# Interleaved B projections, reordered vector work, one gate-weight ring, later transposes and paced FFN loads in an encoder block

One Trainium2 chip, all 8 cores, every core on its own slice of the tokens with the same program. The metric is the device time in microseconds of the slowest core. Every kernel and experiment below gave correct results against the reference.

This program has two states. In the slow one the cores of one die, sometimes of both, run at a visibly lower granted TensorE clock and the time is up to 17% longer.

## The reference

A post-norm encoder block on x of 4 x 4096 x 2048, cut to what matters:

```python
qa, ka, va, qb, kb, vb, ga, gb = jnp.split(x @ w_in, split_pts, axis=-1)
# A: 8 query heads, 2 key/value heads, RMS-normed and rotated, full bidirectional softmax
out_a = _gqa_blocks(qa * scale, ka, va)                       # (B, S, 1024)
# B: 12 heads in 3 groups of dilation 1, 4, 16; 129 keys per query, ALiBi bias;
#    the 3 groups' heads are combined by their softmax denominators
out_b = _dilated_window_attention(qb * scale, kb, vb)         # (B, S, 512)
gate_a = jax.nn.sigmoid(ga + b_gate[0])
gate_b = jax.nn.sigmoid(gb + b_gate[1])
mixed = (gate_a * (out_a @ w_proj_a) + gate_b * (out_b @ w_proj_b)) @ w_out
x = _layer_norm(ALPHA * x + mixed, ln1_g, ln1_b)
h = jax.nn.silu(x @ w_ffn_gate) * (x @ w_ffn_up)              # hidden width 5632
x = _layer_norm(ALPHA * x + h @ w_ffn_down, ln2_g, ln2_b)
```

## The kernel before

The program is written as one list of operations; a helper gives each its waits, and each engine runs its part in list order. So "where a line stands in the list" is the whole schedule. `fil` is a queue of filler matmuls that TensorE takes between the steps of an attention. A matmul writes into one of the program's PSUM banks, and the bank is free again when VectorE or ScalarE has copied its result out ("evacuated" it). A "ring" is a set of buffers taken in turn. A "cold" or half-speed matmul is one that the trace shows at about twice its usual pitch after a gap. The parts, with cuts marked:

```python
# ---- stage 2: attention A (512 steps); filler: B's key, value and query projections
SG = [...4 x [128, 512]...];  KS = at("KS", 184, [128, 3072], BF16)      # staging of values / of keys and queries
def fbank():                       # the filler's two PSUM banks, taken in turn
    b = bank[6 + fb_n[0] % 2]
    fb_n[0] += 1
    return b
def qk_head(wsrc, nt_list, dst, key, dil):         # one key or query head, tiles of 512 tokens
    ...
    s.mm(bk[:, 0:n], w[:, ...], XB_[tb][:, kc, 0:n], kc == 0, kc == 15)
    if kc == 15:
        s.copy("dve", KS[:, tb * 512:tb * 512 + n], bk[:, 0:n])          # cut: the dilated form
        if tb == nt_list[-1][0]:
            s.dma("sp", dst[:, 0:tot], KS[:, 0:tot], wk=[key])           # the store must leave KS before the next head
for g in (2, 1, 0):                                 # four key heads, then all value tiles of the group
    for hh in range(4):
        qk_head(...)
    v_group(g)
...                                                 # then twelve query heads
# at the end of each of the 32 blocks of 16 steps, between filler tiles:
pd = fbank()
s.mm(pd, ones[:, :], AC[blk3 % 2][:, 0:512])        # softmax denominator
s.actf(RD[:, :], pd, AF.Ln)
s.actf(RD[:, :], RD[:, :], AF.Exp, scale=-1.0)
s.tt("dve", QA[h3][:, ...], bank[4 + blk3 % 2], RD[:, :], ALU.mult)

# ---- stage 3: attention B, 48 "quads" (4 per head of dilation 16, then dilation 4 and 1 in turn)
for t in range(NQ + LAGB):
    if t < NQ:
        ... 8 score matmuls into st; bias by VectorE (one or two stt) ...
        ex = s.actf(pb[:, :], st[:, :], AF.Exp)
        pb4 = pb[:, :].rearrange("p (a e c) -> p a e c", a=4, e=2)
        s.tt("dve", DS[t % 3]..., pb4[:, :, 0, :], pb4[:, :, 1, :], ALU.add)      # follows its exp at once
    fil.run_to(min(1.0, (t + 0.5) / NQ))                                          # gate tiles as filler
    if t >= LAGB:
        ... value matmuls of quad t-2 into num, denominators into den ...
        else:                                                                     # dilation 1
            s.tt("dve", ACD[:, cs], den, ACD[:, cs], ALU.add)
            s.tt("dve", ACN[:, cs], num, ACN[:, cs], ALU.add)
            s.actf(ACD[:, cs], ACD[:, cs], AF.Ln)
            s.actf(ACD[:, cs], ACD[:, cs], AF.Exp, scale=-1.0)
            s.tt("dve", OB[hh][:, cs], ACN[:, cs], ACD[:, cs], ALU.mult)          # follows them at once
        if g == 2 and j == 3 and hh < 3:
            load_bq(hh + 1, 2); load_bv(hh + 1, 2)          # next head's queries, keys, bias; values
        if g == 0 and j == 3 and hh < 3:
            load_bq(hh + 1, 1); load_bv(hh + 1, 1); load_bq(hh + 1, 0); load_bv(hh + 1, 0)
    if t < NQ:
        precast_to(NPRE + int((t + 1) * 12 / NQ), ex)       # 12 down-projection pieces, f32 to bf16, DRAM to DRAM

# ---- stage 5: output projection, first norm, transposes for the FFN (16 tiles of 128 tokens)
def p6_ln(tt):                                              # YY and XR: two buffers each
    layer_norm(YY[i], i, LNP)                               # VectorE, then scale and shift on GpSimd
    s.dma("sp", x1_s[...], YY[i][:, :], wk=[("x1", tt)])
    if tt + 2 < 16:
        s.dma("sp", XR[i][:, :], xs_d[(tt + 2) * 128:(tt + 3) * 128, :])
for tt in range(2, 14):
    for fb in range(4):
        wo_mms(tt, fb, bank[fb])
        ...                                                 # the cast of tile 1
        if fb == 1:
            p6_tr(tt - 2)                                   # 16 transposes, evacuated into XTS, stored by pairs
        p6_evac(tt, fb, bank[fb])
    p6_ln(tt); p6_cast(tt)
...
p6_ln(14); p6_cast(14); p6_ln(15); p6_cast(15)

# ---- stage 6: FFN
if not last and (hf, hp) in ((0, 4), (0, 14), (1, 4)):
    ensure_gu(gu_n[0] + 1)                                  # 2 MB of gate and up weights at once
```

The softmax here doesn't subtract the row's maximum and nothing guards it: scores larger than these inputs give would overflow.

Of the kernel before, what the change touches and what calls it, by code (L numbers as in the profile page):

```python
# [325 lines left out]
def build_program():  # L326
# [11 lines left out]
    wka_d = din("wka", [2, 128, 16, 128])  # L338
    wva_d = din("wva", [128, 16, 256])
# [96 lines left out]
    WK = [at("WK", 122 + 4 * i, [128, 16, 128], BF16) for i in range(2)]  # L436
    WV = at("WV", 114, [128, 16, 256], BF16)
# [8 lines left out]
    for k0, k1 in ((0, 1), (1, 2), (2, 4), (4, 8), (8, 12), (12, 16)):  # L446
        s.dma("pool", X[0][:, k0:k1, :], xT_d[0][:, k0:k1, :])
        for i in range(2):
            s.dma("pool", WK[i][:, k0:k1, :], wka_d[i][:, k0:k1, :])
        s.dma("pool", WV[:, k0:k1, :], wva_d[:, k0:k1, :])  # L450
# [144 lines left out]
    early = []  # L595
    for hh in range(2):
        s.dma("pool", WR[hh][:, :], wkb_d[8 + hh].rearrange("p k c -> p (k c)"))
        early.append(WR[hh])
# [6 lines left out]
    PT = [at("PT", 190 + 2 * i, [128, 1024], BF16) for i in range(4)]  # L605
    AC = [at("AC", 198 + 2 * i, [128, 1024], BF16) for i in range(2)]
    SG = [at("SG", (182, 183, 202, 203)[i], [128, 512], BF16) for i in range(4)]
    KS = at("KS", 184, [128, 3072], BF16)
# [4 lines left out]
    wr_n = [0]  # L613
    wq_list = []
# [8 lines left out]
    def wr_load(src):  # L623
        w = WR[wr_n[0] % 5]
        wr_n[0] += 1
        if early:
            return early.pop(0)
        s.dma("pool", w[:, :], src)
        return w

    loads = []
    load_pos = [0]
    slots = {}

    def ensure_loads(n):
        while load_pos[0] < min(n, len(loads)):
            k = load_pos[0]
            slots[k] = wr_load(loads[k])
            load_pos[0] += 1

    def stage_out(bk, dst_list, key):
        g = SG[sg_n[0] % 4]
        sg_n[0] += 1
        s.copy("dve", g[:, :], bk)
        for dst, src in dst_list(g):
            s.dma("sp", dst, src, wk=[key])

    def qk_head(wsrc, nt_list, dst, key, dil):


        li = len(loads)
        loads.append(wsrc)
        tot = sum(n for _, n in nt_list)
        for tb, n in nt_list:
            cell = {}
            for kc in range(16):
                def step(kc=kc, tb=tb, n=n, li=li, cell=cell):
                    if kc == 0:
                        ensure_loads(li + 5)
                        cell["b"] = fbank()  # L660
                    w = slots[li]
                    bk = cell["b"]
                    s.mm(bk[:, 0:n], w[:, kc * 128:(kc + 1) * 128], XB_[tb][:, kc, 0:n], kc == 0, kc == 15)
                    if kc == 15:
                        if dil == 1:
                            s.copy("dve", KS[:, tb * 512:tb * 512 + n], bk[:, 0:n])
                        else:
                            i0 = tb * 512 // dil
                            s.copy("dve", KS[:, 0:tot].rearrange("p (r i) -> p r i", r=dil)[:, :, i0:i0 + n // dil],
                                   bk[:, 0:n].rearrange("p (i r) -> p r i", r=dil))  # L670
                        if tb == nt_list[-1][0]:
                            s.dma("sp", dst[:, 0:tot], KS[:, 0:tot], wk=[key])
                fil.put(max(n, 128) / 512.0, step)

    def v_group(g):
        li = len(loads)
        for q in range(4):
            loads.append(wvb_d[g, q].rearrange("p k c -> p (k c)"))
        dil = B_DIL[g]
        ntile = (17, 18, 24)[g]  # L680
# [11 lines left out]
        for j in range(ntile):  # L692
            cell = {}
            for kc in range(16):
                def step(kc=kc, j=j, cell=cell):
                    if kc == 0:
                        ensure_loads(li + 5)
                        cell["b"] = fbank()
                    w = slots[li + kc // 4]
# [9 lines left out]
    for g in (2, 1, 0):  # L709
        for hh in range(4):  # L710
            hd = g * 4 + hh
            qk_head(wkb_d[hd].rearrange("p k c -> p (k c)"), own + halo[g], kb_s[hd], ("kb", hd), B_DIL[g])
        v_group(g)
    for hh in range(4):
        for g in (2, 0, 1):
            hd = g * 4 + hh
            qk_head(wqb_d[hd].rearrange("p k c -> p (k c)"), own, qb_s[hd], ("qb", hd), B_DIL[g])

    BQ = {2: at("BQ", 130, [128, T], BF16), 0: at("BQ", 150, [128, T], BF16), 1: at("BQ", 166.25, [128, T], BF16)}
    BK = {2: at("BK", 134, [128, 3072], BF16), 0: at("BK", 154, [128, 2112], BF16),  # L720
          1: at("BK", 170.25, [128, 2304], BF16)}
    BV = {2: at("BV", 140, [128, 32, 128], BF16), 0: at("BV", 162, [128, 17, 128], BF16),
          1: at("BV", 174.75, [128, 20, 128], BF16)}
    BB = {2: at("BB", 148, [128, 512], F32), 0: at("BB", 158.1875, [128, 512], F32),
          1: at("BB", 179.75, [128, 512], F32)}

# [22 lines left out]

    LAG = 2  # L750
    NPC = 512
    done_blk = []
    for G in range(NPC + LAG + 2):
        if G < NPC:
# [4 lines left out]
            pt = PT[G % 4]  # L759
# [11 lines left out]
            if G == 440:  # L771
                load_bq(0, 0)
            if pc == 1:
                s.tt("dve", ac[:, :], PT[(G - 1) % 4][:, :], pt[:, :], ALU.add)
# [4 lines left out]
        if G >= LAG and G - LAG < NPC:  # L779
# [4 lines left out]
            for e2 in range(2):  # L784
                c = 2 * pc2 + e2
                s.mm(po, VA[:, c, (h2 // 4) * 128:(h2 // 4 + 1) * 128], PT[g2 % 4][:, e2 * 512:(e2 + 1) * 512],
# [20 lines left out]
    DS = [at("DS", 188 + i, [128, 512], BF16) for i in range(3)]  # L807
    WR3 = [at("WR3", 191 + 4 * i, [128, 16, 128], BF16) for i in range(3)]
# [11 lines left out]
    w3 = {}  # L820
    zn = [0]
    zi = 0
    glist = [(0, f) for f in range(6)]

    def load_w3(i):
        if i < len(glist) and i not in w3:
            ab, f = glist[i]
            w = WR3[i % 3]
            s.dma("pool", w[:, :, :], (wga_d, wgb_d)[ab][f])
            w3[i] = w  # L830

    for i, (ab, f) in enumerate(glist):
        for tb in range(4):
            cell = {}
            for kc in range(16):
                def step(i=i, ab=ab, f=f, tb=tb, kc=kc, cell=cell):
                    if kc == 0:
                        load_w3(i + 1)
                        load_w3(i + 2)
                        cell["b"] = fbank()  # L840
                    s.mm(cell["b"], w3[i][:, kc, :], X[tb][:, kc, :], kc == 0, kc == 15)
# [7 lines left out]
    load_bq(0, 1)  # L849
    load_bv(0, 1)  # L850
    load_bv(0, 0)
    load_w3(0)
    load_w3(1)
# [11 lines left out]
    for t in range(NQ + LAGB):  # L865
        if t < NQ:
# [18 lines left out]
            pb4 = pb[:, :].rearrange("p (a e c) -> p a e c", a=4, e=2)  # L885
            s.tt("dve", DS[t % 3][:, :].rearrange("p (a c) -> p a c", c=128), pb4[:, :, 0, :], pb4[:, :, 1, :], ALU.add)
        fil.run_to(min(1.0, (t + 0.5) / NQ))
        if t >= LAGB:
# [23 lines left out]
            else:  # L912
# [4 lines left out]
                s.tt("dve", OB[hh][:, cs], ACN[:, cs], ACD[:, cs], ALU.mult)  # L917
# [10 lines left out]
    fil.flush()  # L928

# [5 lines left out]
    WGT = [at("WGT", 188 + 4 * i, [128, 16, 128], BF16) for i in range(3)]  # L935
    WPA = [at("WPA", 200 + 2 * i, [128, 8, 128], BF16) for i in range(2)]
    WPB = [at("WPB", 204 + i, [128, 4, 128], BF16) for i in range(2)]
    forder = [6, 0, 7, 1, 8, 2, 9, 3, 10, 4, 11, 5, 12, 13, 14, 15]
    wg_seq = []
    for f in forder:  # L940
        if f >= 6:
            wg_seq.append((0, f))
        wg_seq.append((1, f))
    wg_pos = [0]
    wgm = {}

    def ensure_wg(n):
        while wg_pos[0] < min(n, len(wg_seq)):
            k = wg_pos[0]
            ab, f = wg_seq[k]  # L950
            s.dma("pool", WGT[k % 3][:, :, :], (wga_d, wgb_d)[ab][f])
            wgm[(ab, f)] = WGT[k % 3]
            wg_pos[0] += 1

# [13 lines left out]
    ensure_wg(1)  # L968
    load_wp(0)
    ensure_wg(3)  # L970
    gdone = 0
    for k, f in enumerate(forder):
        wpa, wpb = WPA[k % 2], WPB[k % 2]
        if f >= 6:
            w = wgm[(0, f)]
            gdone += 1
        for tb in range(4):
            tc_ = slice(tb * 512, (tb + 1) * 512)
# [8 lines left out]
            b = nb()  # L987
            for kc in range(8):
                s.mm(b, wpa[:, kc, :], QA[kc][:, tc_], kc == 0, kc == 7)
# [404 lines left out]
```

## Time and profile before

| | us |
|---|---|
| three runs before the prediction | 4344.44, 4351.99, 4571.2 (slow) |
| profiled run, core 1, fast | 4346.5 |

I cut the trace into six stages by TensorE's first matmul of each kind: 1 projections of A; 2 attention A, with B's projections as filler; 3 attention B, with six gate tiles as filler; 4 gates; 5 output projection and first norm; 6 FFN. A stage's "work" is what its matmuls would take back to back at the full-speed pitch that the trace shows (0.2157 us for 128 x 512); the rest of the stage is its "excess". Both stand in the prediction, stage by stage. One border differs: "stage 3" from here on ends with the last denominator matmul (1649.7); the prediction ends it at the first gate tile after it (1658.0), 8 us later. By my border stage 3 lasts 236.4 us with an excess of 100, and stage 4 537.1 with 12.

The profile lines themselves stand in the prediction below.

### The profile page before, as it was taken

Reading aid. Unit: us, or ns where it says so; the run is one execution under the profiler, and the core shown is the slowest. Engines: PE = TensorE matmul, PEld = TensorE weight load, DVE = VectorE, ACT = ScalarE, POOL = GpSimd, SP = SyncE. Lnnn points to the kernel's source line nnn. Section 1 sums busy time; section 2 is a strip of 40 time slices with the busy share of each in tenths; the row PEclk is TensorE's granted clock in tenths of the full one; section 3 lists DMA queues with packets and bytes.
Section 4 is the critical chain, followed back from the end, with each engine's and each line's share of the span. In section 5 each row is a group of like instructions: output and inputs, shape, how many; then the busy total and the mean of one; then the engine's idle time right before and its main releaser. Section 6 shows DMA issues by size and latency. Waiting matters only on the chain.

```text
span 4346.5 us, 50922 instructions; the slowest of 8 cores (4326.0 to 4346.5 us)
## 1 busy us (share of the span) xinstructions
PE 4069.0 (94%) x19504; PEld 1874.6 (43%) x19504; DVE 1286.9 (30%) x1890; ACT 1009.5 (23%) x1229; POOL 496.6 (11%) x434
## 2 busy tenths in 40 slices
PE   7989999989989678999989799999999999999998
PEld 3544444444434343444444344444444444444443
DVE  3564443434434663222245311002110111011104
ACT  1234454545444342111112110001100011001100
POOL 3320000000000000010036300000100010001101
PEclk9999999999999898999999899999999999999999
DMA  9654454444553864444365565354536445544552
GB/s 148 123 96 73 77 92 85 85 84 75 108 106 68 191 158 82 88 96 81 61 208 175 195 203 188 121 194 155 192 128 221 153 168 179 174 150 174 187 196 92
DMA packets 187869, 590.14 MB, mean 136 GB/s; under 512 B 52464, under 2 KB 81072, under 8 KB 157232
## 3 DMA queue, kind: packets, MB, share of 16 engines
q1 hardware_dynamic: 147920, 444.20, 30.3%
q0 software_dynamic: 39712, 142.69, 20.7%
q8 instruction: 160, 2.62, 0.3%
q14 instruction: 77, 0.63, 0.1%
HBM read 659.64 MB, written 147.46 MB: 186 GB/s over the span
## 4 chain that ended last, share of the span: by engine, by line
PE 82%; DMA 7%; DVE 4%; ACT 3%; issue 2%; POOL 1%; SPq 0%; DVEq 0%; ACTq 0%; POOLq 0%
PE pbig L158 82%; DMA kb_s<-KS_112 1%; DVE pbig L190 1%; DMA WD_193<-wfd_s 1%; DMA WD_194<-wfd_s 1%; DMA X_59<-xT 1%; DMA WD_195<-wfd_s 1%; DMA qb_s<-KS_112 1%; DVE KS_112 L194 1%; DVE ACD_131 L178 1%; DMA WV_77<-wva 0%; ACT PT_105 L172 0%; POOL YY_177 L178 0%; POOL YY_178 L178 0%; ACT ACD_131 L172 0%
## 5 line engine op out<-in xcount | busy, mean ns | idle before, releaser
L172 ACT ACTIVATE SGL_205<-pbig 128x512 f32<-128x512 f32 x88 | 52.5, 597 | 952.5 <-PE pbig L158 952.3
L178 DVE TENSOR_TENSOR HT_192<-SGL_206,pbig 128x512 bf16<-128x512 f32 x88 | 60.5, 687 | 529.7 <-PE pbig L158 529.7
L158 PE MATMUL pbig<-WD_193,HT_192 128*128 128x512 bf16 x832 | 196.6, 383 | 8.9 <-DMA WD_193<-wfd_s 8.3
L178 DVE TENSOR_TENSOR HT_192<-SGL_205,pbig 128x512 bf16<-128x512 f32 x88 | 60.5, 688 | 486.2 <-PE pbig L158 468.5
L158 PE MATMUL pbig<-WD_194,HT_192 128*128 128x512 bf16 x816 | 190.8, 381 | 8.1 <-DMA WD_194<-wfd_s 7.8
L158 PE MATMUL pbig<-WD_195,HT_192 128*128 128x512 bf16 x816 | 190.3, 379 | 8.1 <-DMA WD_195<-wfd_s 7.8
L172 ACT ACTIVATE SGL_206<-pbig 128x512 f32<-128x512 f32 x88 | 52.5, 597 | 505.3 <-PE pbig L158 505.3
L190 DVE SCALAR_TENSOR_TENSOR YY_154_196<-XR_158_200,pbig 128x512 f32<-128x512 f32 x16 | 11.0, 688 | 534.8 <-PE pbig L158 534.8
L172 ACT ACTIVATE PT_104<-pbig 128x1024 bf16<-128x1024 f32 x128 | 131.1, 1024 | 159.4 <-PE pbig L158 106.4
L172 ACT ACTIVATE PT_103<-pbig 128x1024 bf16<-128x1024 f32 x128 | 131.1, 1024 | 150.8 <-PE pbig L158 116.2
L178 POOL TENSOR_TENSOR YY_154_196<-YY_154_196,LNP_162_204 128x2048 f32<-128x2048 f32 (+1 forms) x10 | 32.4, 3240 | 1152.7 <-DVE YY_154_196 L185 998.3
L172 ACT ACTIVATE PT_102<-pbig 128x1024 bf16<-128x1024 f32 x128 | 131.1, 1024 | 128.5 <-PE pbig L158 70.1
L172 ACT ACTIVATE PT_105<-pbig 128x1024 bf16<-128x1024 f32 x128 | 130.5, 1020 | 98.8 <-PE pbig L158 76.3
L158 PEld LDWEIGHTS pbig<-WD_193,HT_192 128*128 128x128 bf16 x832 | 81.3, 99 | 111.4 <-issue 17.1
L158 PEld LDWEIGHTS pbig<-WD_194,HT_192 128*128 128x128 bf16 x816 | 79.7, 98 | 107.4 <-issue 13.9
L158 PEld LDWEIGHTS pbig<-WD_195,HT_192 128*128 128x128 bf16 x816 | 79.2, 98 | 106.2 <-issue 11.8
L158 PE MATMUL pbig<-X1T_184,WG_187 128*128 128x512 bf16 x448 | 104.2, 387 | 19.4 <-ACT SGL_205 L172 19.4
L158 PE MATMUL pbig<-X1T_184,WU_191 128*128 128x512 bf16 x480 | 108.5, 379 | 0.0
L158 PE MATMUL pbig<-X1T_184,WG_186 128*128 128x512 bf16 x480 | 108.5, 379 | 0.0
L158 PE MATMUL pbig<-X1T_184,WU_189 128*128 128x512 bf16 x480 | 108.5, 379 | 0.0
L158 PE MATMUL pbig<-X1T_185,WG_186 128*128 128x512 bf16 x480 | 108.5, 379 | 0.0
L158 PE MATMUL pbig<-X1T_185,WU_189 128*128 128x512 bf16 x480 | 108.5, 379 | 0.0
(830 smaller groups left out, 7322.1 us busy)
## 6 DMA issues: line engine op xcount, KB each, us to landing
WG_186<-wfg_s SPq DMA_DIRECT2D x30, 1024.0 KB
WU_189<-wfu_s SPq DMA_DIRECT2D x30, 1024.0 KB
WG_187<-wfg_s SPq DMA_DIRECT2D x29, 1024.0 KB
WU_190<-wfu_s SPq DMA_DIRECT2D x29, 1024.0 KB
WG_188<-wfg_s SPq DMA_DIRECT2D x29, 1024.0 KB
WU_191<-wfu_s SPq DMA_DIRECT2D x29, 1024.0 KB
WD_193<-wfd_s SPq DMA_DIRECT2D x52, 512.0 KB
WD_194<-wfd_s SPq DMA_DIRECT2D x51, 512.0 KB
```

Source lines behind the costliest of these rows:

```text
L158: fn = lambda e: e.matmul(out, lhsT=lhsT, rhs=rhs, start=start, stop=stop)
L172: return self.add("act", lambda e: e.activation(out=out, in_=in_, func=func, **kw), ins, [out])
L178: return self.add(eng, lambda e: e.tensor_tensor(out=out, in0=a, in1=b, op=op), [a, b], [out])
L190: return self.add("dve", lambda e: e.scalar_tensor_tensor(out=out, in0=a, scalar=sc, in1=b, op0=op0, op1=op1), ins, [out])
L194: return self.add(eng, lambda e: e.tensor_copy(out=out, in_=in_), [in_], [out])
```

## The change

Its intent, by stage: (1) keys' and values' weights of A as one array; (2) key heads of B alternate with value tiles so that the staging buffer KS is stored while other tiles run, query heads get two halves of KS, the staging ring SG of the values grows from 4 to 5, and the exponential ring shrinks from 4 to 3 to pay for it; (3) VectorE adds the halves of a quad's exponentials and forms the product OB one quad later, when ScalarE has finished; (3, 4) one ring of gate weights across both stages; (5) transposes one tile later, with a fourth buffer XBF; (6) two casts moved into the FFN, weights fetched in pieces of 0.5 MB, residual tiles one by one. The diff, cut to its core:

```diff
-    KS = at("KS", 184, [128, 3072], BF16)
+    KS = at("KS", 184, [128, 4096], BF16)
-    PT = [at("PT", 190 + 2 * i, [128, 1024], BF16) for i in range(4)]
+    PT = [at("PT", 192 + 2 * i, [128, 1024], BF16) for i in range(3)]
 ...
-    for g in (2, 1, 0):
-        for hh in range(4):
-            qk_head(...)
-        v_group(g)
+    for gi, g in enumerate((2, 1, 0)):
+        ...                                        # nseg = 3 or 4 cuts of the group's value tiles
+        for i in range(nseg):
+            v_tiles(g, cuts[i], cuts[i + 1])
+            ...
+            k_head(g, hh)
+    for q, hd in enumerate(qorder):
+        ...
+        qk_head(WR[(q + 1) % 5], own, qb_s[hd], ("qb", hd), B_DIL[hd // 4], 2048 * ((q + 1) % 2))
 ...
+    WGT = [at("WGT", 188 + 4 * i, [128, 16, 128], BF16) for i in range(3)]      # one gate ring, from stage 2 on
 ...
+            if G == 504:
+                ensure_wg(1)
 ...
-    WR3 = [at("WR3", 191 + 4 * i, [128, 16, 128], BF16) for i in range(3)]
 ...
-            pb4 = pb[:, :].rearrange("p (a e c) -> p a e c", a=4, e=2)
-            s.tt("dve", DS[t % 3][:, :]..., pb4[:, :, 0, :], pb4[:, :, 1, :], ALU.add)
-        fil.run_to(min(1.0, (t + 0.5) / NQ))
+        if 1 <= t <= NQ:
+            pb4 = PB[(t - 1) % 3][:, :].rearrange("p (a e c) -> p a e c", a=4, e=2)
+            s.tt("dve", DS[(t - 1) % 3][:, :]..., pb4[:, :, 0, :], pb4[:, :, 1, :], ALU.add)
+        while late_ob:
+            late_ob.pop(0)()
+        fil.run_to(min(1.0, (t + 0.5) / (NQ + 1)))
 ...
-                s.tt("dve", OB[hh][:, cs], ACN[:, cs], ACD[:, cs], ALU.mult)
+                late_ob.append(lambda hh=hh, cs=cs: s.tt("dve", OB[hh][:, cs], ACN[:, cs], ACD[:, cs], ALU.mult))
 ...
-            if fb == 1:
-                p6_tr(tt - 2)
+            if fb == 1 and tt >= 3:
+                p6_tr(tt - 3)
 ...
-            p6_tr(12, (2, 6, 3, 7))
+            p6_tr(11, (2, 6, 3, 7))
             load_x1T(0)
         else:
             ensure_gu(fb)
+        if fb == 1:
+            p6_tr(12, (2, 6, 3, 7))
     p6_ln(14)
-    p6_cast(14)
     p6_ln(15)
-    p6_cast(15)
 ...
+            if tb == 0 and j in (2, 3):
+                p6_cast(12 + j)
 ...
-                if not last and (hf, hp) in ((0, 4), (0, 14), (1, 4)):
-                    ensure_gu(gu_n[0] + 1)
+                if not last and hp in ((1, 4, 7, 10, 13, 16), (4, 7, 10, 13, 16, 18))[hf]:
+                    ensure_gp(gu_n[0] + 1)
+                if hf == 1 and hp in (1, 3, 6, 9):
+                    load_xr(tb, 1, ((1, 3, 6, 9).index(hp),))
```

## The prediction

> **What bounds the kernel now.** I read the page first, then the busy time by stretch with cuts at the stage borders, then TensorE's waits stage by stage, then the timelines round the worst waits. The profile is of core 1, 4346.5 us, in the fast state (dies at 0.978 and 0.980). The two fast runs mean 4348, the third (4571.2) I take for slow.
>
> ```profile
> PE 4069.0 (94%) x19504; PEld 1874.6 (43%) x19504; DVE 1286.9 (30%) x1890; ACT 1009.5 (23%) x1229; POOL 496.6 (11%) x434
> PE   7989999989989678999989799999999999999998
> PEclk9999999999999898999999899999999999999999
> ```
>
> TensorE sets the time, so only its idle time can be won. The tenths show where that lies: slices 1, 3, 12, 14 to 16, 21 and 23. Busy time hides part of it, since modelled ends stretch each matmul over the next. So I count instead. Streams of 128x512 matmuls start 0.2157 us apart in the timeline; scaled by columns, a 128x128 one is 0.056. The program's matmuls per stage times these are the work; the rest is excess:
> 1 projections of A, 0 to 272: work 232, excess 40.
> 2 attention A with B's projections as filler, 272 to 1413: work 1021, excess 120.
> 3 attention B with six gate tiles as filler, 1413 to 1658: work 136, excess 109.
> 4 gates, 1658 to 2187: work 525, excess 4.
> 5 output projection and first norm, 2187 to 2446: work 233, excess 27.
> 6 FFN, 2446 to 4346.5: work 1826, excess 74.
> In all 3972 of work and 374 of excess. The next rows are the stretches of stages 2, 3 and 4: length, then busy time of PE, PEld, DVE, ACT, POOL, granted clock, DMA share, GB/s. In stage 3 the clock falls to 0.88, and DVE's 153 us is more than TensorE's 136 of work.
>
> ```profile
> 272.30:1413.30 1141.00, 1054.04 (x4817) 470.42 (x4816) 475.30 (x724) 559.89 (x576) 75.44 (x141) 0.97 0.48 86
> 1413.30:1658.00 244.70, 166.79 (x1202) 91.11 (x1202) 153.36 (x198) 97.40 (x122) 11.32 (x23) 0.88 0.71 163
> 1658.00:2186.80 528.80, 527.43 (x2433) 238.46 (x2434) 132.03 (x192) 88.08 (x129) 44.40 (x85) 1.00 0.43 86
> ```
>
> TensorE's waits name the causes: total, times, longest. KS is the staging of B's keys and queries, ACN the sum that value matmuls wait for, SGL the first FFN evacuation, WR_96 and WGT gate weights.
>
> ```profile
> PE pbig L158 <- DVE KS_112 L194: 59.9, 32, 7.5
> PE pbig L156 <- DVE ACN_130 L178: 43.6, 24, 2.4
> PE pbig L158 <- ACT SGL_205 L172: 19.4, 1, 19.4
> ...
> PE pbig L158 <- ACT XBF_179 L175: 12.2, 1, 12.2
> PE pbig L158 <- DMA WR_96_138<-wga: 10.2, 1, 10.2
> ...
> PE pbig L158 <- DMA WGT_164<-wga: 7.9, 1, 7.9
> ```
>
> **What the Trainium skill says.** "TensorE: Matmul & The Clock Gate", section "Architectural detail", calls VectorE and ScalarE strict FIFO. The trace agrees: in stage 3 DVE idles 1.22 us before every add of the halves of the exponentials (DS), waiting for ACT, with other work queued behind it. Its section "HAM oscillation" says gaps over about 3.4 us drop TensorE to half rate. After the 7.46 us gap at 326.2 the next matmuls are about 0.43 us apart for some 5 us, so a long stall costs about 2 us more than itself. "DMA: Bandwidth & Descriptors", section "Issuing engines are not separate DMA queues", says all transfers share 16 engines; "Why small descriptors are slow" bears on the value tiles' 256-byte rows. Here the five BV_122 transfers (128 KB each) hold the queue from 1538.55 to 1545.66.
>
> **Part by part. Stage 1:** keys' and values' weights become one array: 12 fewer issues of some 0.55 us on GpSimd, and longer rows. But the first block ends at 49 us when its bytes have come, and they are the same bytes. Estimate: 3 us.
>
> **Stage 2:** a key head's first copy waits until the previous head's store has left KS:
>
> ```profile
> DVE KS_112 L194 <- DMA kb_s<-KS_112: 30.6, 8, 5.7
> DVE KS_112 L194 <- DMA qb_s<-KS_112: 20.8, 9, 6.2
> ```
>
> Alternation puts 4 to 8 value tiles between two key heads. A tile takes 16 filler matmuls at about 5.2 per step of 2.0 us, 6.2 us, so the store has 25 to 50 us. Query heads get two halves of KS. This wait goes. But 59.9 us is not the gain. In the pure value phase (441 to 598) the excess is still 7.5% of the time, in the other two 9 to 10.5%, against 13, 12 and 11.5% in key phases and 10.6% in the query phase. Its stalls come at each of the 32 block ends, every 33 us: the denominator's matmul takes one of the two filler banks, so the next tile must wait for the copy of the one just ended, behind DVE's 1.3 to 2.0 us wait for the reciprocal (RD). The change leaves that. With 8.4%, the mean of the value phases with the key leftovers at 955 to 968 taken out, stage 2 is 1021/0.916 = 1114 instead of 1141: 27 us. The exponential ring shrinks from 4 to 3; DVE's add follows an exponential by 0.1 us, so that is free once DVE is not held up by stores.
>
> **Stage 3**, the largest part. DVE now, one pair of quads:
>
> ```profile
> 1455.65 1.23 DVE L190 SCALAR_TENSOR_TENSOR pbig<-pbig,BB_125 128x1024 f32<-128x1024 f32 x1
> 1458.10 0.42 DVE L178 TENSOR_TENSOR DS_137<-PB_134 128x512 bf16<-128x512 bf16 x1 [1.22 <-ACT PB_134 L172]
> 1458.44 1.05 DVE L178 TENSOR_TENSOR ACN_130<-pbig,ACN_130 128x512 f32<-128x512 f32 x1
> 1459.39 1.07 DVE L178 TENSOR_TENSOR ACD_131<-pbig,ACD_131 128x512 f32<-128x512 f32 x1
> 1460.37 1.22 DVE L190 SCALAR_TENSOR_TENSOR pbig<-pbig,BB_124 128x1024 f32<-128x1024 f32 x1
> 1462.81 0.43 DVE L178 TENSOR_TENSOR DS_135<-PB_132 128x512 bf16<-128x512 bf16 x1 [1.22 <-ACT PB_132 L172]
> 1463.15 0.69 DVE L178 TENSOR_TENSOR ACD_131<-pbig,ACD_131 128x512 f32<-128x512 f32 x1
> 1463.75 0.68 DVE L178 TENSOR_TENSOR ACN_130<-pbig,ACN_130 128x512 f32<-128x512 f32 x1
> 1465.45 0.69 DVE L178 TENSOR_TENSOR OB_126<-ACN_130,ACD_131 128x512 bf16<-128x512 f32 x1 [1.02 <-ACT ACD_131 L172]
> ```
>
> DS and the OB product move one quad later, when ACT has long finished; the idle 1.22 and 1.02 us go. From start to start DVE then needs, for a quad of dilation 4, 1.2 + 0.34 + 0.95 + 0.98 = 3.47; of dilation 1, 1.2 + 0.34 + 0.6 + 0.6 + 0.61 = 3.35; of dilation 16, 1.2 + 0.34 + 0.9 = 2.44. TensorE needs 0.45 + 0.45 + 0.22 and 8 filler matmuls, 1.73: 2.85. DVE bounds the first two kinds, TensorE the third: 16 x (3.47 + 3.35 + 2.85) = 155. Gate weights are now fetched from step 504 of stage 2 and stay in one ring, so 10.2 and 7.9 us go; stage 4 starts with four gate tiles (13.8 us) over its other weights. Start and tail: 6. New wait: the next head's loads have about 6 us before dilation 4 needs them and 10 before dilation 1 does, where they had 11.7 and 15; the dilation 1 keys took about 16 from the first issue. Estimate: 4 us at each of three heads, 12. Stage 3: 173 instead of 245, 72 less; I count 68 for cold matmuls.
>
> **Stage 4:** 4 us of excess, 1 won. **Stage 5:** transposes one tile later take away the 12.2 us wait for XBF_179 and about 2 of cold matmuls. At the end three waits for XTS (7.5 in all) stay in some form: two transposes now follow each other within 6.9 us, and the single XTS must first be stored. 13 us.
>
> **Stage 6:** the 19.4 us at 2479 is ACT standing at two casts behind GpSimd's norm (two 4.5 us operations per tile), with the first silu behind them. The casts move to blocks 2 and 3, 27.6 and 41 us in; gone. The other term is down-projection weights queued behind 2 MB of gate and up weights, or behind four residual loads:
>
> ```profile
> 2854.31 0.38 SPq L148 DMA_DIRECT2D XR_158_200<-x_s  x1
> ...
> 2856.34 0.76 SPq L148 DMA_DIRECT2D WD_193<-wfd_s  x1
> ```
>
> These WD waits add to 31 with their cold matmuls over three blocks. Paced in 0.5 MB pieces, about 6 stay (the two last weights of a half are needed together, 1.2 us each time). 20 + 25 = 45.
>
> Sum: 3 + 27 + 68 + 1 + 13 + 45 = 157. 4348 - 157 = 4191; I say 4195.
>
> **Rivals.** (a) Loads bound stage 3. For: its DMA share is 0.71 already, and the same bytes in 173 us ask for about 1.0; the 256-byte rows are slow. Against: some transfers overlap in that share, and one gate weight leaves. Then 200 to 215 there: 4225 to 4235. (b) KS was only the name of the last releaser, and all stage 2 stalls are block ends, also for query heads, whose excess is 10.6%: it gains 10 or less, 4212. (c) Block ends fall better once DVE never waits for a store, stage 2 runs at 7.5% or less and no new load wait comes: 40 there and 80 in stage 3, 4166. (d) New order makes new stalls: transposes 11 and 12 back to back, or TensorE idling into half clock in DVE-bound quads (0.6 us of idle each, too short I think): plus 10 to 20.
>
> **Range and chances.** The excess of 374 caps the gain; some 93 of stage 2 (1114 - 1021) and 37 of stage 1 remain by design. Stage 3 is uncertain by 25, stage 2 by 15, the others by 10: together about 40. Range 4150 to 4245. Over 2% faster needs below 4261, which fails only if stage 3 and another part both fail: 0.93.
>
> **What would show it.** Right: no KS store wait on DVE, stage 2 near 1114 with waits on SG and KS every 33 us; stage 3 near 173 with no ACT wait before DS, DVE busy near 90%, clock near 0.95; no wait for WR_96 or WGT; stage 5 near 246; no SGL wait; WD waits under 8. Wrong: BK or BQ waits over 15 us in stage 3, waits for XTS over 10, or a stage 2 still over 1130.

## The result

The changed kernel ran four times: 4244.16 and 4242.95 fast, 4800.1 and 4743.64 slow. The kernel before in the same rounds: 4339.9, 4344.44 and 4351.99 fast, 4571.2 slow. All outputs are right. Ratios in this document are the mean of one kernel's fast runs over that of the other's in the same rounds, so not quite the ratio of medians: 0.9766, 95% interval 0.9733 to 0.9798. That is **104 us faster, where 153 were predicted**. The fast time, 4243, lies at the upper edge of the range. What has to be explained is the missing 50 us.

The page of the changed kernel, core 7, 4242.3 us (busy time, then the tenths by slice and the granted clock):

```profile
PE 4036.3 (95%) x19504; PEld 1868.3 (44%) x19504; DVE 1284.3 (30%) x1890; ACT 1007.3 (24%) x1229; POOL 491.2 (12%) x422
PE   7999999999999779999989899999999999999998
PEclk9999999999999899999999999999999999999999
```

The FFN (the last 17 slices) has no dent left but its last slice, which had it before; the dents that stay are slice 1, the two of stage 3 and those of stage 5. By my count of stages, on the slowest core of each profiled run:

| stage | before | after | gain | predicted gain |
|---|---|---|---|---|
| 1 | 272.3 | 265.9 | 6.4 | 3 |
| 2 | 1141.0 | 1114.0 | 27.0 | 27 |
| 3 and 4 | 773.5 | 740.4 | 33.1 | 69 |
| 5 | 259.3 | 271.5 | -12.2 | 13 |
| 6 | 1900.4 | 1850.6 | 49.8 | 45 |
| sum | 4346.5 | 4242.3 | 104.2 | 157 |

Stages 3 and 4 are added because the prediction's border between them differs. The cores of one run differ too: stage 2 lasts 1131 to 1141 us before and 1110 to 1117 after, stage 3 232 to 236 and 207 to 215, stage 5 254 to 265 and 267 to 272. A few us between two single cores are therefore no finding. Two misses make the difference: 36 us in stage 3, 25 us in stage 5. TensorE's waits after the change (total, times, longest):

```profile
PE pbig L158 <- DVE KS_110 L194: 45.7, 29, 2.6
PE pbig L158 <- DMA BK_117<-kb_s: 27.4, 4, 12.6
...
PE pbig L158 <- ACT XTS_179 L175: 12.8, 3, 5.5
PE pbig L158 <- DVE YY_172 L190: 11.8, 1, 11.8
...
PE pbig L158 <- DMA BK_116<-kb_s: 8.2, 3, 4.2
PE pbig L158 <- DVE XTS_179 L194: 7.4, 1, 7.4
PE pbig L158 <- ACT PB_134 L172: 6.1, 1, 6.1
```

Of VectorE's waits for a store to leave KS, 51.4 us before, one is left:

```profile
DVE KS_110 L194 <- DMA kb_s<-KS_110: 6.6, 1, 6.6
```

Against the list of TensorE's waits in the prediction: SGL, XBF, WR_96 and WGT are gone, the ACN sum fell from 43.6 to 3.3. In their place stand keys of B that are not yet loaded (BK_117 is dilation 1, BK_116 dilation 4), the evacuation of a tile in stage 5 (YY), and XTS, which was 4.9 and 2.6 before. The busy time by stretch shows stage 3 from another side (length, then busy time of PE, PEld, DVE, ACT, POOL, granted clock, DMA share, GB/s):

```profile
1379.80:1594.40 214.60, 157.61 (x1201) 88.91 (x1201) 148.56 (x195) 94.61 (x120) 11.42 (x22) 0.89 0.81 184
```

DVE is now busy 69% of the stage, not the 90% that I gave as the sign of success, and the clock stayed at 0.89. And yet VectorE does just what was intended. Its timeline in stage 3, one quad of dilation 4 and one of dilation 1 (start, length, operation):

```profile
1473.90 1.26 DVE L190 SCALAR_TENSOR_TENSOR pbig<-pbig,BB_122 128x1024 f32<-128x1024 f32 x1
1475.03 0.45 DVE L178 TENSOR_TENSOR DS_137<-PB_134 128x512 bf16<-128x512 bf16 x1
...
1477.91 1.33 DVE L190 SCALAR_TENSOR_TENSOR pbig<-pbig,BB_123 128x1024 f32<-128x1024 f32 x1
...
1480.57 1.33 DVE L190 SCALAR_TENSOR_TENSOR pbig<-pbig,BB_122 128x1024 f32<-128x1024 f32 x1
```

The 1.22 us of idle time ahead of DS are gone, and a pair of quads takes 6.67 us from start to start, where the prediction worked out 3.47 + 3.35 = 6.82. So the missing time is not in the steady state; it is at the changes of head.

### The profile page after: what moved, and what is told of

Its sections match the earlier page's. It is cut to its first block, busy times and chain, and to the rows that moved or that the text cites. A ratio compares the mean times of both kernels' runs of the same rounds, so it can differ in the third digit from the quotient of the medians.

```text
span 4242.3 us, 51519 instructions; the slowest of 8 cores (4230.0 to 4242.3 us)
## 1 busy us (share of the span) xinstructions
PE 4036.3 (95%) x19504; PEld 1868.3 (44%) x19504; DVE 1284.3 (30%) x1890; ACT 1007.3 (24%) x1229; POOL 491.2 (12%) x422
## 4 chain that ended last, share of the span: by engine, by line
PE 87%; DMA 4%; DVE 3%; issue 2%; ACT 2%; SPq 1%; POOL 1%; DVEq 0%; POOLq 0%; ACTq 0%
PE pbig L158 87%; SPq L148 1%; DMA X_59<-xT 1%; DMA BK_117<-kb_s 1%; DVE ACD_132 L178 0%; DVE KS_110 L194 0%; ACT PT_101 L172 0%; ACT PT_100 L172 0%; DVE pbig L190 0%; ACT PT_102 L172 0%; DMA x1T_s<-XTS_179 0%; DMA WO_166<-wo_s 0%; DMA WD_189<-wfd_s 0%; DMA BB_123<-bbias 0%; DMA WD_191<-wfd_s 0%
## 5 line engine op out<-in xcount | busy, mean ns | idle before, releaser
L158 PE MATMUL pbig<-WD_189,HT_188 128*128 128x512 bf16 x832 | 194.1, 379 | 2.7 <-DMA WD_189<-wfd_s 2.1
L158 PE MATMUL pbig<-WD_191,HT_188 128*128 128x512 bf16 x816 | 190.3, 379 | 1.5 <-DMA WD_191<-wfd_s 1.2
L158 PE MATMUL pbig<-WD_190,HT_188 128*128 128x512 bf16 x816 | 189.2, 379 | 0.9 <-DMA WD_190<-wfd_s 0.4
L178 POOL TENSOR_TENSOR YY_150_192<-YY_150_192,LNP_158_200 128x2048 f32<-128x2048 f32 (+1 forms) x10 | 32.4, 3241 | 1107.3 <-DVE YY_150_192 L185 952.9
L158 PE MATMUL pbig<-X1T_180,WG_184 128*128 128x512 bf16 x480 | 108.5, 379 | 0.0
L158 PE MATMUL pbig<-X1T_180,WU_185 128*128 128x512 bf16 x480 | 108.5, 379 | 0.0
L158 PE MATMUL pbig<-X1T_181,WU_186 128*128 128x512 bf16 x480 | 108.5, 379 | 0.0
L158 PE MATMUL pbig<-X1T_181,WG_183 128*128 128x512 bf16 x480 | 108.5, 379 | 0.0
L158 PE MATMUL pbig<-X1T_181,WG_182 128*128 128x512 bf16 x480 | 108.5, 379 | 0.0
L158 PE MATMUL pbig<-X1T_181,WU_185 128*128 128x512 bf16 x480 | 108.5, 379 | 0.0
L158 PE MATMUL pbig<-X1T_180,WG_182 128*128 128x512 bf16 x480 | 108.5, 379 | 0.0
```

What stands on the lines that cost most here:

```text
L158: fn = lambda e: e.matmul(out, lhsT=lhsT, rhs=rhs, start=start, stop=stop)
L178: return self.add(eng, lambda e: e.tensor_tensor(out=out, in0=a, in1=b, op=op), [a, b], [out])
```

## The experiments

Runs came in three batches; the first two were on one chip, the last (c_ffn_old, c_yb, b_den, a_best2) on another, where the kernel before took 4360 to 4370 and many cores had a lower clock (0.96 to 0.98), above all in stage 2. There I compare ratios, waits, and stage 2 only on cores with a clock of 0.99 in it.

**b_vec: the reordered vector work alone, on the kernel before.**

```diff
-            s.tt("dve", DS[t % 3]..., ...)
+        if 1 <= t <= NQ:  s.tt("dve", DS[(t - 1) % 3]..., ...)      # and late_ob, as in the change
```

> The kernel before, with only the new order of the vector work in attention of group B (value tiles, gate ring, transposes, loads as before). If VectorE's order is what bounded stage 3 before and ScalarE's results come in time once the order is changed, stage 3 falls from 236 us to about 210 or less (gain 25 or more), and waits for loads of 15 us or more come to the fore. If the alternation of keys with values is needed for it (the loads otherwise come too late), stage 3 gains under 12 us. No other stage moves by more than 8 us.

Stage 3 was 210.7 us, 25.7 less than before and about as short as the 214.6 of the whole change (203 to 211 on the eight cores, against 207 to 215). The only fast run was 4315.35 (before in the same rounds 4337.64 to 4347.77). TensorE's waits in stage 3:

```profile
PE pbig L158 <- DMA BK<-kb_s: 30.8, 6, 8.4
PE pbig L158 <- DMA WR<-wga: 9.2, 1, 9.2
```

So the order of VectorE's work was what bounded stage 3, it alone brings the gain, and the waits for keys come with it; the new order of the projections did not make them.

**Three ways to free those keys.** Each was run on the changed kernel. *a_order*: the keys of dilation 1 ahead of the values of dilation 4.

```diff
                 load_bq(hh + 1, 1)
-                load_bv(hh + 1, 1)
                 load_bq(hh + 1, 0)
+                load_bv(hh + 1, 1)
                 load_bv(hh + 1, 0)
```

> The changed kernel, where at the same moment queries and keys of both groups are issued ahead of the values of both (only the order changes). If the dilation 1 keys wait because value rows of 256 bytes stand ahead in the queue (about 5 us for each of three heads): the waits for BK_117 fall from 28 to 10 to 15 us, stage 3 from 214 to about 198. If collisions with the GpSimd queue's transfers cause them: less than 6 us change. If issued too late: between.

*a_early*: queries, keys and bias of the next head right after the last score matmuls that read them, two or three quads earlier; values as soon as their last reader is done.

```diff
             ex = s.actf(pb[:, :], st[:, :], AF.Exp)
+            if j == 3 and hh < 3:
+                load_bq(hh + 1, g)
 ...
-            if g == 2 and j == 3 and hh < 3:  load_bq(hh + 1, 2); load_bv(hh + 1, 2)
-            if g == 0 and j == 3 and hh < 3:  load_bq(hh + 1, 1); ...; load_bv(hh + 1, 0)
+            if j == 3 and hh < 3:
+                load_bv(hh + 1, g)
```

> The changed kernel, where the next head's queries, keys and biases of a group are loaded as soon as its last score matmuls are issued (dilation 4 and 1: three and two quads sooner), and its values after its last value matmuls. In the changed kernel the waits for BK are 37 us and stage 3 takes 214 us. If the loads are merely issued too late: waits for BK under 8 us, stage 3 175 to 185 us, kernel 25 to 40 us less. If they collide with other transfers wherever they fall: waits of at least 15 us stay.

*a_noprecast*: the twelve weight conversions that ran during stage 3 are moved to stage 4.

```diff
-            precast_to(NPRE + int((t + 1) * 12 / NQ), ex)
+            pass
 ...
-        precast_to(NPRE + 12 + int((k + 1) * (len(pre) - NPRE - 12) / 16), sg)
+        precast_to(NPRE + int((k + 1) * (len(pre) - NPRE) / 16), sg)
```

> The changed kernel, where none of the 12 conversions of down-projection weights (DRAM to DRAM, 32 KB packets of about 4.5 us on each of the 16 engines) runs in stage 3; they are moved to stage 4. If such a packet on every engine stops the loads: the waits for BK fall from 37 us by 12 to 18, stage 3 from 214 to about 197. If order or lateness is the cause: by less than 5 us. Either way stage 4 stays within 2 us of 512 plus its first tile.

| stage 3, profiled run | length | excess due to waits for BK | for BV | clock | fast runs |
|---|---|---|---|---|---|
| changed kernel | 214.6 | 36.8 | 0 | 0.89 | 4242.95, 4244.16 |
| a_order | 201.2 | 14.4 | 8.7 | 0.91 | 4232.18, 4233.17, 4236.02 |
| a_early | 191.6 | under 1 | 9.0 | 0.94 | 4223.84 |
| a_noprecast | 186.6 | 16.8 | 0 | 0.94 | 4222.2, 4226.3, 4228.52 |

The ratios to the kernel before are 0.9721 (0.9672 to 0.9771) for a_order and 0.9703 (0.9652 to 0.9753) for a_noprecast. a_order came out as expected. a_early freed the keys, but the stage stayed 7 us above the 175 to 185 expected, because the values are waited for instead. a_noprecast gained more than expected. All three help: the order of loads, their time of issue and the conversions each hold part of the wait, and no single one is its cause. The largest single effect is that of the conversions, 28 us. The DMA view of the changed kernel from 1448.5 to 1453.5, just after the keys' load was issued at 1447.07, shows how (share and GB/s in 40 slices, a packet counted where it starts, then the queues):

```profile
DMA  1389949999900000000000000000000000000131
GB/s 47 88 199 461 369 111 633 854 1333 559 533 0 0 0 0 0 0 0 0 0 0 0 0 0 0 0 0 0 0 0 0 0 0 0 0 0 0 33 33 66
...
q0 software_dynamic: 17, 0.52, 91.2%
q1 hardware_dynamic: 504, 0.14, 12.4%
```

One conversion of 0.5 MB (queue q0) consists of 16 packets of 32 KB, one on each DMA engine, and each takes about 4.5 us here (the twelve conversions of stage 3 have medians of 2.4 to 4.6); the keys and values (q1) move nothing for some 3 us of these 5. The Trainium skill, "DMA: Bandwidth & Descriptors", section "Queues, rings and completion order", says that an engine takes its queues in turn and drains a whole packet of one before it turns to the next. The trace agrees, and shows the price: a turn of 4.5 us, against 0.16 us for a 4 KB packet of the keys.

**a_den: the bank of the denominator matmul in stage 2.** The prediction said that the stalls at the 32 block ends stay because that matmul takes one of the filler's two banks out of turn. This takes it out of the count:

```diff
-                pd = fbank()
+                pd = bank[6 + fb_n[0] % 2]
```

> The changed kernel, where the denominator's matmul of attention A borrows the filler bank that the next tile would take, instead of using one up. Theory: at each of the 32 block ends the next filler tile is sent to the bank of the tile just ended and waits for its copy, 1.4 to 2.9 us each; then stage 2 falls from 1114.0 us to 1050 to 1075, the waits on KS and SG from 74 us to under 30, and the kernel by 40 to 60 us. Rival: the stall is DVE standing at the reciprocal (RD), whatever the bank; then stage 2 changes by less than 10 us.

Stage 2 fell from 1114.0 to 1044.8, more than expected (1043 to 1045 on all eight cores), its excess from 93 to 24; the fast runs were 4173.8, 4176.85 and 4173.88, ratio 0.9586 (0.9537 to 0.9635). TensorE's waits there:

```profile
PE pbig L158 <- DVE KS L194: 10.3, 9, 1.7
...
PE pbig L158 <- DVE SG L194: 3.8, 3, 1.3
```

KS went from 45.7 to 10.3. The stalls came from the bank that the next filler tile had to take, not from VectorE's load.

**b_den: the same edit on the kernel before.**

> The kernel before with only the bank of the denominator matmul changed. The same edit on the changed kernel gained 69 us of stage 2. If the waits for KS behind its store and the block ends are separate, stage 2 falls here by about the same, from 1141 to about 1072, and the KS waits that stay (25 us or more) are those behind the stores: then the 27 us that the change gained in stage 2 are the stores. If the stores hide under the block ends, stage 2 falls to about 1050 and the alternation of heads and value tiles would have been worth little.

Fast runs 4272.39, 4288.52, 4293.69 and 4295.02, ratio 0.9825 (0.9798 to 0.9852): faster, though whether by 2% is unclear. On the four cores whose clock in stage 2 was 0.99 or more it lasted 1047 to 1055 us. That is the outcome I had listed as the rival: with the bank put right, the old order of the projections is within some 10 us of the new one (a_den, 1045), although VectorE still waits for the stores of KS as long as ever (core 3):

```profile
DVE KS L194 <- DMA kb_s<-KS: 35.0, 8, 7.2
DVE KS L194 <- DMA qb_s<-KS: 20.6, 7, 5.5
```

(Core 3 had a clock of 0.97 in stage 2; on core 6, at 1.00, the two sums are 28.1 and 21.1.) These some 50 us of VectorE cost TensorE little: it waits for KS 16.3 us on core 6, against 10.3 in a_den. The likely reason is that it has a second bank to go on with. So the alternation of key heads and value tiles was worth 27 us only in company of the badly placed bank. In the other order, by medians of the cores and across two chips, the bank is worth some 85 us (1137 to 1053) and the alternation some 8 (1053 to 1045).

**c_ffn_old: both edits of the FFN undone in the changed kernel.**

```diff
-            if tb == 0 and j in (2, 3):  p6_cast(12 + j)          # casts 14 and 15 again ahead of the FFN
-                if not last and hp in ((1, 4, ...), (4, 7, ...))[hf]:  ensure_gp(gu_n[0] + 1)
+                if not last and (hf, hp) in ((0, 4), (0, 14), (1, 4)):  ensure_gp(gu_n[0] + 4)
+            if hf == 1:  load_xr(tb, 1)                           # four residual tiles at once
```

> The changed kernel with both edits of the feed-forward stage undone: the casts of tiles 14 and 15 stand again ahead of the first silu, gate and up weights come again in 2 MB lots and the four residual tiles at once. If the 20 + 25 of the prediction were sized rightly, the wait for SGL comes back with 19 us or so, the WD waits rise from 4.8 to about 27, and stage 6 from 1850 to about 1895; no other stage moves by more than 4 us. If the gate-weight ring or the earlier stages had brought part of it, one of the two stays under half.

Stage 6 grew to 1903 to 1913 us on the eight cores (1850.6 in the changed kernel); the fast runs were 4332.8 and 4330.17, the ratio to before is 0.9926 (0.9904 to 0.9947). TensorE waits 19.2 us for SGL and 32.4 for WD, as against 0 and 3.7. Both sizes hold, WD rather more than expected.

**a_tr12: one transpose fewer at the end of stage 5.**

```diff
-        if fb == 1:
-            p6_tr(12, (2, 6, 3, 7))
-    late_tr = [13, 14, 15]
+    late_tr = [12, 13, 14, 15]
-            if tb == 0 and j in (3, 4, 5):
+            if tb == 0 and j in (2, 3, 4, 5):
```

> The changed kernel, with transpose 12 moved back from the start of stage 5's last stretch into the feed-forward stage (at the second gate tile), so that only 13 to 15 are late. If TensorE's waits for the transposes' store (21 us in stage 5: 13.4 on ScalarE, 7.7 on VectorE) come from too many late transposes standing close together, they fall to 6 us or less and stage 5 from 271.5 to about 255, the whole by about 15 us, to 4228. Rival: the waits come from the norm's chain of tile 2 and 3 (the load of the x tile behind the store), and moving a transpose does not touch that: stage 5 stays over 266.

The excess due to XTS fell from 21.1 to 8.8 us and stage 5 from 271.5 to 263.3, but 6.1 us came up as a wait for the first FFN weights (1853.1 in stage 6). The two fast runs, 4240.37 and 4242.35, are hardly faster, since on the slowest core the other stages took 6 us more; the medians of the dies, 4230.5 and 4229.3, are some 7 us below those of the changed kernel (4237.9 and 4236.0). So the back-to-back transposes hold part of the XTS waits. They are not the whole cause: a_xr, next, leaves them as they are and takes away almost as much.

**a_xr: the load of the residual tile ahead of the norm instead of behind the store.**

```diff
+        if tt + 2 < 16:
+            s.dma("sp", XR[i][:, :], xs_d[(tt + 2) * 128:(tt + 3) * 128, :])
         layer_norm(YY[i], i, LNP)
         s.dma("sp", x1_s[tt * 128:(tt + 1) * 128, :], YY[i][:, :], wk=[("x1", tt)])
-        if tt + 2 < 16:
-            s.dma("sp", XR[i][:, :], xs_d[(tt + 2) * 128:(tt + 3) * 128, :])
```

> The changed kernel, with the load of the residual tile issued ahead of the norm and the store of x1 instead of behind them. If the load behind the store is what holds the evacuation of tile 2 (TensorE waits 11.9 us at 2173 for VectorE's YY_172), that wait falls under 3 us and the waits at the end fall too, stage 5 from 271.5 to about 255. Rival: the ring of two YY buffers holds it (a buffer is free only after norm, store and cast): 8 us or more of the wait stay, named ZS or YY instead of XR.

Stage 5 was 260.0, 11.5 less, most of it from the end: the XTS waits fell from 20.2 to 11.3, and fewer matmuls ran at half speed. The fast runs were 4231.49, 4235.32, 4235.97, ratio 0.9749 (0.9727 to 0.9771). But the wait for YY stayed at 10.5. In the changed kernel its last releaser is the load (VectorE's timeline, then SyncE's issues):

```profile
2167.65 0.16 DVE L1037 RECIPROCAL RS_55<-RS_55 128x1 f32<-128x1 f32 x1 [8.35 <-ACT RS_55 L172]
2167.92 1.35 DVE L185 TENSOR_SCALAR YY_173<-YY_173,MV_53,RS_55 128x2048 f32<-128x2048 f32 x1
2172.78 2.48 DVE L190 SCALAR_TENSOR_TENSOR YY_172<-XR_170,pbig 128x512 f32<-128x512 f32 x4 [3.51 <-DMA XR_170<-xs]
```

```profile
2165.44 0.33 SPq L148 DMA_DIRECT2D x_s<-YY_172  x1
2165.81 0.43 SPq L148 DMA_DIRECT2D XR_170<-xs  x1
```

The store of tile 0 and the load behind it are issued together. By the semaphores in the trace the store has landed at 2170.15 and the load at 2172.62, so the load held the evacuation 2.5 us longer than the store. In a_xr the store is the last releaser: it landed 6.0 us after its issue in place of 4.7, again with a residual load (the next tile's) issued right behind it. So the rival held: two releasers stand close together, and the profile names the later. Why the store took longer was not tested.

**c_yb: a_xr, and a shorter way to a free YY.** Scale and shift of tiles 0 and 1 go to VectorE, and tile 2 uses the banks of tile 1.

```diff
-        layer_norm(YY[i], i, LNP)
+        layer_norm(YY[i], i, LNP, "dve" if tt < 2 else "pool")     # engine of the two tensor_tensor
-            wo_mms(tt, fb, bank[fb])
+            b = bank[fb + (4 if tt == 2 else 0)];  wo_mms(tt, fb, b)
-            if fb == 1 and tt >= 3:  p6_tr(tt - 3)
+            if fb == 1 and tt >= 4:  p6_tr(tt - 3)
+            if fb == 3 and tt == 3:  p6_tr(0)
```

> Stage 5 with the residual load ahead of the norm (which alone gained 11 us there but left the wait for YY at 10.7), and besides the scale and shift of tiles 0 and 1 on VectorE instead of GpSimd, and tile 2 in the PSUM banks that tile 1 used. If the wait for YY is the chain from the last evacuation of tiles 0 and 1 through norm, scale and shift on GpSimd and store (about 23 us) against the 14 us of TensorE's work between, it falls from 10.7 to 5 or less and stage 5 from 260 to about 254. Rival: the single waits only move on to tile 4 and the transposes; stage 5 stays at 258 or more.

The wait for YY fell to 3.2 us and stage 5 to 254.9 on the slowest core, but only to 257 in the median of the cores (255 to 259, against 259 to 262 in a_xr), between what I expected and what the rival said: XTS took back 2.4 us. The fast runs were 4253.31 to 4271.81 on the second chip, ratio 0.9768 (0.9746 to 0.979), so the whole does not show these few us beside that chip's slower stage 2. The two operations took 4.51 and 4.49 us on GpSimd in a_xr and 2.29 us each on VectorE here. That is what the Trainium skill, "GPSIMD Engine Reference", section "Elementwise — side-by-side cycle accounting", gives for an addition of 2048 elements of float32 (4497 and 2293 ns).

Two edits were made at once, and the fall can't be put down to the shorter chain alone. From the start of the stage, the first evacuation of tile 2 comes at 50.8 us against 52.0 in a_xr, hardly earlier, because VectorE has the norm of tile 1 in front of it. That of tile 3 comes at 58.7 against 64.9. And with tile 2 in other banks TensorE does one more tile (64 matmuls, 13.8 us) before it needs a bank back. By these figures either edit alone would have left some 9 us of the wait (an estimate); no run separates them.

**a_best: a_den, a_early, a_noprecast, a_tr12 and a_xr together.**

> The changed kernel with five edits together: the denominator in a bank pair that alternates with the feed-forward's count, earlier query and key loads, the twelve conversions of weights out of stage 3, transpose 12 earlier, the residual load earlier. If the gains add: stage 2 about 1045 (from 1114), stage 3 about 175 to 185 (from 215; early loads and no conversions overlap in effect), stage 5 about 255 (from 271.5), stages 4 and 6 plus 2: in all 4243 - 69 - 35 - 15 + 2 = about 4126 (4110 to 4150). If the early loads and the absence of conversions act on the same waits only, stage 3 stays at 187 or more and the total is over 4140.

Fast runs 4123.6 and 4129.66, ratio 0.9501 (0.9473 to 0.9529): it beats both kernels, by some 117 us the changed one. Stage 2 took 1047.4, stage 5 257.9, and stage 3 166.1, better than expected. No load is among TensorE's waits there any more:

```profile
1314.10:1480.20 166.10, 146.27 (x1177) 84.91 (x1201) 147.77 (x195) 94.08 (x120) 5.26 (x10) 0.98 0.76 200
```

VectorE is busy 89% of the stage and the clock is at 0.98, near the signs the prediction named for stage 3. Was it bandwidth that bounded the changed kernel? The 16 DMA engines were busy for 174 us of its stage 3 (share 0.81 of 214.6). a_early has the same transfers there, and they took 172 us (0.90 of 191.6). So bandwidth did not set the 214.6. But if the packets keep that time, they fill all of the 173 us that were predicted (an estimate from these shares). a_best goes below because the conversions have left the stage: 0.76 of 166.1 is 126.

**a_best2: a_best with the edits of c_yb.**

> The combined version (4128 in its profiled run) with the three edits of stage 5 from the run before this in it. If they gain in stage 5 as there, 257.9 falls to about 250 and the whole to about 4118; if the end of stage 5 is bound by the x tiles' other chains, it stays within 3 us of 4126.

Fast runs 4148.49, 4150.34 and 4158.33 on the second chip, ratio 0.9518 (0.9495 to 0.9541): the same as a_best within the intervals, so the 4118 expected was not reached, on a chip with a slower stage 2. In its profile stage 5 lasts 248.3 us on the core with the best clock and 255.7 on the slowest; a gain of 8 us in the whole is neither shown nor excluded.

## Why the prediction was right in parts and too high in sum

**Stage 2: the right number by half a reason.** 1114 was predicted and measured; that it fits so closely is luck (the cores range from 1110 to 1117, and the 8.4% that it rests on includes stretches of key matmuls: with the borders set by the matmuls themselves the three value phases have 7.5, 8.3 and 7.5% of excess, which gives 1107). The step "this wait goes, but 59.9 us is not the gain" was right, and so was the cause given for the stalls at the block ends (a_den). What b_den adds is that the 27 us are not a property of the store: most of them arise only while the block ends cost TensorE its second bank. That a store making VectorE late is then what hurts is argued; the runs show that the two do not add. The prediction took them for independent terms.

**Stage 3: the failed term is the one for late loads.** The step was "Estimate: 4 us at each of three heads, 12". In the changed kernel the waits for keys cost 36.8 us, 25 too many. At the heads' changes the single gaps were 12.56 us at the first, 2.73 + 8.18 at the second and 4.23 + 4.81 at the third, not 4 each. The estimate set about 10 us of time until the dilation 1 keys are needed against "about 16 from the first issue" until they land, and that 16 was read in the slower kernel before (15.3 to 16.6 there, by the semaphores in the trace). The time until need was not the error: it came out as 12.4, 13.9 and 12.7. The landing was: 24.7, 21.8 and 17.2 us after the first issue. Of these, 10.2, 12.7 and 9.8 pass before SyncE issues the keys at all. Most of that goes to the five transfers of dilation 4 values in front of them (6.2, 9.6 and 6.6 us to issue), which the prediction had seen in the kernel before and did not work out anew, and which a_order moves. And at each of the three heads a conversion starts within 2 us of that issue (1449.0, 1503.3, 1555.0), which the prediction did not look at and a_noprecast moves.

Most of the rest is a term that was not in the sum: 7.6 us at the start, most of it because ScalarE cannot write PB_134 before the last query head has been stored from KS, which lies over it. In the kernel before, the 10.2 us wait for the gate weight WR_96, booked as gain, stood at this same place (until 1424.1). What remains are short waits and half-speed matmuls after the gaps. The main term, VectorE's pitch, was right: 6.67 us a pair against 6.82. And with the loads out of the way a_best's stage of 166 us comes out under the 173 predicted, though without the conversions. The prediction's rival (a), "200 to 215 there", describes the result (214.6): loads did bound the stage, but by when they land and not by bandwidth, which was its reason. For the 173 itself its "about 1.0" was not refuted (see a_best).

**Stage 5: the sign was wrong.** The 12.2 us wait for XBF did go. An 11.8 us wait for YY took its place, because both hung on one chain: tile 0's norm is done about 17 us after its last evacuation, and cast, store and next residual load all start there (2165.4). The wait was moved from the transposes to the next output tile, and the step that failed is that 12.2 us was booked as gain without asking what the freed TensorE meets next. At the end, "three waits for XTS (7.5 in all) stay in some form" was under-sized: 20.2 us. Transposes 11 and 12 follow each other and the one buffer must be stored between, which is part of it (a_tr12 leaves 8.2); but the place of the residual load is another part (a_xr leaves 11.3). The first is the prediction's own rival (d); I put it at plus 10 to 20 and did not weigh it in.

**Stages 1, 4 and 6.** Stage 6 gained 50 where 45 was said, and c_ffn_old puts both terms back. Stage 1's 6 instead of 3 is within what single cores differ by. Stage 4 lost its gate-weight wait as expected. A slip without consequence: after the 7.46 us gap at 326.2, thirteen matmuls come 0.38 to 0.43 us apart, so that stall costs 2.7 us more than itself, not about 2.

**Open.** The three edits for stage 3 gain 13 (a_order), 23 (a_early) and 28 us (a_noprecast) singly. a_best, which has the last two, gains 49, so these two nearly add up; how a_order overlaps with them was not taken apart further.

## What to carry to other kernels

When a stage's bound engine is made faster, first list everything that the old pace had left time for: buffer reuse, loads issued at the head change, background copies. Each of these is a new candidate for the end of the wait, and its size comes from what stands ahead of it and beside it in just that window. And a wait that the profile names is a name for the last releaser: before its length is booked as gain, ask which second releaser stands right behind it, and whether the waiting engine had a second buffer that made the wait free anyway.

## What the Trainium skill lacked or had wrong

- "DMA: Bandwidth & Descriptors", section "Queues, rings and completion order", has the turn-taking at packet granularity, but not how long such a turn can be. Here a DRAM-to-DRAM conversion of 0.5 MB put one 32 KB packet on each of the 16 engines for about 4.5 us, and the other queue's data stood still for some 3 us.
- "TensorE: Matmul & The Clock Gate", section "HAM oscillation", goes by waits that outlast a window (about 3.4 us). Here the gap's length alone did not tell: in the kernel before, a gap of 2.86 us before 885.25 was followed by seven matmuls 0.33 to 0.43 us apart (the trace has the clock at half from 884.58 to 887.99), and one of 3.94 us before 3333.99 by matmuls at full pitch (0.2157).
- No page puts a number on what a wait of VectorE costs TensorE behind two PSUM banks in turn. In b_den 55.6 us of such waits went with 18.3 us of TensorE waiting for KS (49.2 with 16.3 on another core).
